# Toeplitz stage of an S5 layer: steps of four groups instead of two, state copies moved behind the low parts, and more column products behind the scan

## The chip, the cores and the metric

One NeuronCore of a Trainium2 chip runs the whole layer in one launch. The metric is the device time in microseconds (us) of an execution; the profile belongs to one such execution. PE is the matrix engine, DVE the vector engine, ACT the scalar engine, POOL the GpSimd engine and SP the engine that issues most DMAs.

## The reference

A bidirectional encoder layer over 2 sequences of 512 tokens, 1024 wide. A projection yields queries, keys, values, the state-space input u and two gates. The attention branch is windowed; the state-space branch (S5) runs a diagonal complex recurrence with 64 states for each of 64 groups of 16 channels, forwards and backwards, and applies GELU and a gated linear unit; then both are merged and a squared-ReLU MLP follows. The part that matters here:

```python
def one_direction(us, d, reverse):
    bu_re = jnp.einsum('lgc,gpc->lgp', us, bb_re[d])
    bu_im = jnp.einsum('lgc,gpc->lgp', us, bb_im[d])
    ...
    _, _, h_re, h_im = lax.associative_scan(_complex_combine, (ar, ai, bu_re, bu_im),
                                            reverse=reverse, axis=0)
    return (jnp.einsum('lgp,gcp->lgc', h_re, cr[d])
            - jnp.einsum('lgp,gcp->lgc', h_im, ci[d]))
...
y = one_direction(ug, 0, False) + one_direction(ug, 1, True)
y = jax.nn.gelu(y.reshape(seq_len, SSM_WIDTH) + dsk * uf)
```

## The kernel before

The recurrence is cut into chunks of 8 tokens. In a first stage (the tables) the kernel builds, for every group, a Toeplitz matrix that maps the 128 inputs of a chunk (16 channels x 8 tokens) to its outputs, and two tables of 128 columns (real and imaginary) that map the states at a chunk's edges to the outputs. Tables go to DRAM (`ct_scr`, L522, with 9 column blocks of 16, of which the Toeplitz stage uses 8; `lag_scr`, from which `toep_scr` is made). Then the scan walks over the 64 chunks on DVE (L602 to L605). Then comes the **Toeplitz stage**, with the loop that the change rewrites.

Before the change this loop has 32 turns `q`, each for two groups (`SH` = 2), which share one PSUM bank:

- PE: for each group one product of the Toeplitz matrix with the inputs (L642) and two of the tables with the states (L645). In the trace each of these f32 products is two records, so a turn has 12 of them.
- The states are copied out of the scan's array `h` into a tile `st`, in the order that the products read. `state_rows(q)` copies the partitions 64 to 127 on DVE (L613), and 0 to 63 on ACT for even q (L615) or on DVE for odd q (L617). There are three `st` buffers, and turn q makes the states of turn q + 2.
- ACT: GELU of the bank (L655), then the rounding to the matmul format, the high part (L621). DVE: the low part, the difference (L622). In the code the low part and the store of a turn stand one turn later, behind the state copies of that turn (`remainder`, `full`).
- ACT issues the stores of both parts to `y_scr` (L626) after every four groups (`SI` = 4). The part tiles have two buffers each, so a high part needs the store of two stores ago landed.
- POOL issues the loads: the state tables of four groups (L590, three buffers), and u and the Toeplitz matrices of eight groups (`SB` = 8; L582 and L584, two buffers).

On PE, ACT and DVE the code's order is the queue's order here (`manual_schedule`); POOL's and SP's order is chosen by a scheduler. Into PE's queue the kernel weaves **fillers**: products of the other projections, which are needed later. `pull(n)` takes n units of them. A product of a column block, L185, is worth two units, 24 make one result of 128 x 512; ACT copies that result out (L200), ACT rounds pieces of the next weights (L175, `c_hi`), and DVE forms their low parts (L176, `c_lo`). When the columns are done, the key products follow: L225, one unit each, 24 for one tile of 128 tokens. Such a tile is squared on ACT (L232), summed on DVE (L234), turned into a scale on POOL (L236, L237) and scaled on DVE (L238). A result is taken out of PSUM at the place in ACT's and DVE's order where its last product was pulled.

Each step of the scan pulls 15 units; behind the scan stands `pull(32)`; each turn of the Toeplitz loop pulls its share of what is left over 84 units; and after the loop comes the rest. After that the attention stage begins with products that need weights from SP (L980, L981, L813).

Of the kernel before, what the change touches and what calls it, by code (L numbers as in the profile page):

```python
# [12 lines left out]
F32 = mybir.dt.float32  # L13
F32R = mybir.dt.float32r
I32 = mybir.dt.int32
AF = mybir.ActivationFunctionType
# [3 lines left out]
P = 128  # L20
# [5 lines left out]
NSEQ = 2  # L26
# [12 lines left out]
GROUPS = 64  # L39
STATE = 64  # L40
CH = 16
T = 8
NCHUNK = SEQ // T
SB = 8
SI = 4
SG = 4
SH = 2
# [16 lines left out]
def hybrid_layer(ctx, tc, x, rel, onehot, w_qkv, w_ug, vectors, lam, coefs, w_glu, w_out, ln2,  # L64
                 w_up, w_down, out):
    nc = tc.nc
    V, S, PE, GP, SP = nc.vector, nc.scalar, nc.tensor, nc.gpsimd, nc.sync
# [4 lines left out]
    dram = ctx.enter_context(tc.tile_pool(name="dram", bufs=1, space=DRAM))  # L72
# [19 lines left out]
    ct_scr = dram.tile([P, GROUPS, 2, 9 * CH], F32, name="ct_scr")  # L92
# [58 lines left out]
    phase = {"next": 0, "raw": [], "units": 2 * 3 * KT * NSEQ * len(columns) + 3 * KT * NT, "gelu": False}  # L151
# [119 lines left out]
    with tc.tile_pool(name="xin", bufs=1, reuse_waits="tile") as xin, tc.tile_pool(name="ssmc", bufs=1) as sc:  # L271
# [148 lines left out]
        ps = ps_o.tile([P, 512], F32, tag="po", name="line")  # L420
# [21 lines left out]
    with tc.tile_pool(name="hst", bufs=1) as hp:  # L442
# [11 lines left out]
        with tc.tile_pool(name="ssmt", bufs=2) as sp:  # L454
# [9 lines left out]
            def tables(c):  # L464
# [22 lines left out]
                for q in range(SB // SG):  # L487
                    g0 = c * SB + q * SG
# [20 lines left out]
                    for ri, t in enumerate((bi_p, br_p)):  # L509
# [5 lines left out]
                    ctab = sp.tile([P, SG, 2, 9, CH], F32, tag="ctab", name="ctab")  # L515
# [3 lines left out]
                    V.tensor_sub(ctab[:, :, 0], tb, ctab[:, :, 0])  # L519
                    V.tensor_mul(ctab[:, :, 1], bc_pow(er, 9), bc_ch(cw[:, 1], 9))  # L520
                    V.tensor_sub(ctab[:, :, 1], ctab[:, :, 1], tb)
                    GP.dma_start(ct_scr[:, g0:g0 + SG].rearrange("p g r n -> p (g r n)"),  # L522
                                 ctab.rearrange("p g r n c -> p (g r n c)"))
# [54 lines left out]
        with tc.tile_pool(name="ssmo", bufs=2) as sp:  # L578
            def load_batch(g0):

                u_sb = sp.tile([P, SB, NSEQ * NCHUNK], F32, tag="u_sb", name="u_sb")
                GP.dma_start(u_sb, u_scr[g0:g0 + SB].rearrange("g c t k -> (c t) g k"))  # L582
                toep = sp.tile([P, SB, T, CH], F32, tag="toep", name="toep")
                GP.dma_start(toep.rearrange("p g t c -> p g (t c)"),  # L584
                             toep_scr[:, :, g0:g0 + SB].rearrange("c t g n -> (c t) g n"))
                return u_sb, toep

            def load_table(g0):
                ctab = sp.tile([P, SI, 2, 9 * CH], F32, tag="ctab", name="ctab_in", bufs=3)
                GP.dma_start(ctab.rearrange("p g r n -> p (g r n)"),  # L590
                             ct_scr[:, g0:g0 + SI].rearrange("p g r n -> p (g r n)"))
                return ctab

            ahead = [load_batch(0)]
            ahead_c = [load_table(0), load_table(SI), load_table(2 * SI)]
            ahead.append(load_batch(SB))
            GP.dma_start(line_scr, line_one[:, None, :].to_broadcast([N_HEADS, P, LINE]))
            order.close()
            order.enter_context(tc.manual_schedule(engines={mybir.EngineType.PE, mybir.EngineType.Activation, mybir.EngineType.DVE}))
            for i in range(1, NCHUNK - 1):  # L600
                t1, t2 = [sp.tile([P, 2, GROUPS, NSEQ], F32, tag="st", name=n, bufs=3) for n in ("t1", "t2")]
                V.tensor_mul(t1, h[:, i], a8r)  # L602
                V.tensor_mul(t2, h[:, i, ::-1], a8i)
                V.tensor_add(t1, t1, h[:, i + 1])
                V.tensor_add(h[:, i + 1], t1, t2)  # L605
                pull(15)
            phase["gelu"] = True
            pull(32)
            def state_rows(q):
                st = sp.tile([P, 2, SH, NSEQ, NCHUNK], F32, tag="st", name="st", bufs=3)  # L610
                hv = h[:, :, :, q * SH:(q + 1) * SH, :].rearrange("p k r g s -> p r (g s) k")
                sv = st.rearrange("p r g s k -> p r (g s) k")
                V.tensor_copy(sv[64:128], hv[64:128, :, :, ::-1])  # L613
                if q % 2 == 0:
                    S.copy(sv[0:64], hv[0:64])  # L615
                else:
                    V.tensor_copy(sv[0:64], hv[0:64])  # L617
                return st

            def rounded(y, parts, g):  # L620
                S.copy(parts[0][:, g:g + SH, :], y)  # L621
                return lambda: V.tensor_sub(parts[1][:, g:g + SH, :], y, parts[0][:, g:g + SH, :].bitcast(F32))  # L622
# [7 lines left out]
            remainder = full = None  # L630
            for q in range(GROUPS // SH):
                g0 = q * SH
                if g0 % SB == 0:
                    u_sb, toep = ahead.pop(0)
                if g0 % SI == 0:
                    ctab = ahead_c.pop(0)
                    ysp = [sp.tile([P, SI, NSEQ * NCHUNK], F32R, tag=f"y{n}", name=f"y{n}") for n in ("hi", "lo")]
                st = states.pop(0)
                ps = sps()
                for g in range(SH):  # L640
                    o = ps[:, g * P:(g + 1) * P]
                    PE.matmul(o, toep[:, g0 % SB + g].rearrange("p t c -> p (t c)"), u_sb[:, g0 % SB + g, :],  # L642
                              start=True, stop=False)
                    for ri in range(2):
                        PE.matmul(o, ctab[:, g0 % SI + g, ri, 0:T * CH],  # L645
                                  st[:, ri, g].rearrange("p s k -> p (s k)"), start=False, stop=ri == 1)
# [8 lines left out]
                S.activation(yg.rearrange("p g k -> p (g k)"), ps[:, 0:SH * P], AF.Gelu_apprx_tanh)  # L655
                remainder = rounded(yg, ysp, g0 % SI)
                if (g0 + SH) % SI == 0:
                    full = ysp, g0 + SH - SI

                pull(-(-(phase["units"] - 84) // (GROUPS // SH - q)))  # L660
                if (g0 + SH) % SI == 0 and g0 + SH + 2 * SI < GROUPS:
                    ahead_c.append(load_table(g0 + SH + 2 * SI))
                if (g0 + SH) % SB == 0 and g0 + SH + SB < GROUPS:
                    ahead.append(load_batch(g0 + SH + SB))
            remainder()
            store_y(*full)
            pull(phase["units"])
            order.close()

# [66 lines left out]
    with tc.tile_pool(name="att", bufs=2, reuse_waits="tile") as ap, tc.tile_pool(name="attc", bufs=1, reuse_waits="tile") as ac:  # L736
# [289 lines left out]
        with tc.manual_schedule(engines={ET.PE, ET.Activation, ET.DVE, ET.Pool}):  # L1026
            for i, (j, sq) in enumerate(steps):
# [152 lines left out]
    with tc.tile_pool(name="glu", bufs=1, reuse_waits="tile") as gpool, \  # L1180
# [10 lines left out]
        for u in range(2, 2 * KT):  # L1191
            m, s = divmod(u, 2)
# [206 lines left out]
    with tc.tile_pool(name="up", bufs=2, reuse_waits="tile") as fp:  # L1399
# [26 lines left out]
        for r in range(NPAIR):  # L1426
# [40 lines left out]
    with tc.tile_pool(name="downb", bufs=1, side="right", reuse_waits="tile") as db, \  # L1467
# [47 lines left out]
        ps = product_d(1)  # L1515
# [5 lines left out]
        ps = product_d(5)  # L1521
# [5 lines left out]
        ps = product_d(6)  # L1527
# [3 lines left out]
        ps = product_d(3)  # L1531
# [4 lines left out]
        ps = product_d(7)  # L1536
# [5 lines left out]
        ps = product_d(2)  # L1542
# [3 lines left out]
        ps = product_d(4)  # L1546
# [82 lines left out]
```

## Time and profile before

| What | us |
|---|---|
| median of 3 runs | 1474.6 |
| the runs | 1472.87 to 1474.95 |
| the profiled execution, its own time | 1474.1 |
| span of that execution in the trace | 1472.3 |
| scan (L602 to L605) in the trace | up to 323.3 |
| Toeplitz products (L642, L645) in the trace | 326.7 to 411.4 |
| last key product (L225) | about 422.4 |

A span begins with the first and ends with the last recorded instruction; the time holds what lies around it too. In lists of instructions the first number is the start in us from the span's start, the second the duration in us; "x4" counts records that were merged, and "[1.81 <-ACT st L615]" is idle time of the engine just before, with what ended it. In groups by line the columns are the line, engine and operation, output and inputs with shape and count, then busy us, mean ns, idle time in front and its causes. Matmuls are pipelined: the record of a matmul ends later than the start of the next.

### The profile page before, as it was taken

The page shows a single profiled execution, that of the slowest core. Times are in us where ns is not written, and L with a number is a line of the kernel's source. Part 1 is how long each engine was busy: PE and PEld are TensorE (multiplying, and loading weights), DVE is VectorE, ACT ScalarE, POOL GpSimd, SP SyncE. Part 2 cuts the span into 40 slices and gives each one's busy share as a digit, 9 for nine tenths or more (in the row PEclk, how much of TensorE's full clock was granted, in tenths as well). Part 3 has the DMA queues.
Part 4 walks back from the last instruction along what each step waited for, and adds up shares of the span by engine and source line. Part 5 has one row for each costly group of instructions (what it writes and reads, how often), then busy time and mean ns, then how long its engine had stood idle before and what let it go on. Part 6 is the DMA issues. An engine that isn't in the chain of part 4 may idle for free.

```text
span 1472.3 us, 22141 instructions
## 1 busy us (share of the span) xinstructions
PE 1442.3 (98%) x8074; PEld 1230.4 (84%) x8074; DVE 1101.7 (75%) x1989; ACT 760.0 (52%) x1362; POOL 210.4 (14%) x372
## 2 busy tenths in 40 slices
PE   6999999999999999999999999999999999999998
PEld 4788888879899999998888878888888888888787
DVE  7998859986645899997984588777776597475553
ACT  6677762225535888776343355544544444333332
POOL 3133351002322444222100000000000000000000
PEclk9999999999999999999999999999999999999999
DMA  4455459328940445367553244444443893454441
GB/s 177 142 172 172 165 167 362 116 100 299 346 163 16 144 151 158 107 234 232 191 193 114 86 157 175 148 153 145 146 150 115 326 338 108 158 184 146 127 129 58
DMA packets 102877, 249.16 MB, mean 169 GB/s; under 512 B 12234, under 2 KB 23754, under 8 KB 102768
## 3 DMA queue, kind: packets, MB, share of 16 engines
q1 hardware_dynamic: 60240, 139.55, 29.2%
q0 software_dynamic: 16896, 53.53, 10.5%
q10 hardware_dynamic: 25632, 54.67, 9.9%
q8 instruction: 64, 1.05, 0.3%
q14 instruction: 45, 0.37, 0.1%
HBM read 173.22 MB, written 90.21 MB: 179 GB/s over the span
## 4 chain that ended last, share of the span: by engine, by line
PE 82%; DVE 7%; ACT 4%; DMA 3%; issue 3%; POOL 1%; ACTq 0%; SPq 0%; DVEq 0%; POOLq 0%
PE acc L185 14%; PE bank L117 14%; PE bank L118 13%; PE bank L116 13%; PE acc L813 5%; PE acc L123 3%; PE acc L117 2%; PE acc L118 2%; PE acc L116 2%; PE po L896 2%; PE sps L864 2%; PE sps L547 2%; PE tps L880 2%; PE acc L835 1%; PE sps L645 1%
## 5 line engine op out<-in xcount | busy, mean ns | idle before, releaser
L185 PE MATMUL acc<-act,c_hi 128*128 128x512 f32 x768 | 250.5, 401 | 1.0 <-DVE act L304 0.9
L117 PE MATMUL bank<-b_lo,a_hi 128*128 128x512 f32 x448 | 174.6, 390 | 1.4 <-DVE b_lo L1498 1.4
L118 PE MATMUL bank<-b_hi,a_lo 128*128 128x512 f32 x448 | 174.3, 389 | 0.0
L116 PE MATMUL bank<-b_hi,a_hi 128*128 128x512 f32 x448 | 173.5, 389 | 0.0
L185 PEld LDWEIGHTS acc<-act,c_hi 128*128 128x128 f32 x768 | 142.6, 190 | 29.2 <-DVE act L304 2.4
L185 PE MATMUL acc<-act,c_lo 128*128 128x512 f32 x384 | 153.2, 399 | 0.0
L1497 ACT CAST a_hi<-d_a 128x1024 fp32r<-128x1024 f32 x56 | 59.0, 1054 | 179.3 <-PE bank L117 177.7
L116 PE MATMUL bank<-act,act 128*128 128x512 f32 x368 | 143.3, 389 | 0.5 <-ACT f_sum L1322 0.5
L117 PE MATMUL bank<-act,act 128*128 128x512 f32 x368 | 143.3, 389 | 0.2 <-DVE act L1281 0.2
L118 PE MATMUL bank<-act,act 128*128 128x512 f32 x368 | 143.2, 389 | 0.0
L1498 DVE TENSOR_TENSOR a_lo<-d_a,a_hi 128x1024 fp32r<-128x1024 f32 x56 | 68.5, 1224 | 99.7 <-ACT a_hi L1497 99.7
L813 PE MATMUL acc<-w_hi,act 128*128 128x256 f32 x512 | 114.2, 291 | 0.0
L117 PEld LDWEIGHTS bank<-b_lo,a_hi 128*128 128x128 f32 x448 | 84.1, 188 | 19.6 <-DVE b_lo L1498 2.4
L116 PEld LDWEIGHTS bank<-b_hi,a_hi 128*128 128x128 f32 x448 | 84.1, 188 | 17.6
L118 PEld LDWEIGHTS bank<-b_hi,a_lo 128*128 128x128 f32 x448 | 84.1, 188 | 17.4
L813 PEld LDWEIGHTS acc<-w_hi,act 128*128 128x128 f32 x512 | 87.1, 190 | 3.7
L185 PEld LDWEIGHTS acc<-act,c_lo 128*128 128x128 f32 x384 | 72.8, 190 | 14.0 <-DVE c_lo L176 0.5
L116 PEld LDWEIGHTS bank<-act,act 128*128 128x128 f32 x368 | 69.1, 188 | 15.3 <-ACT f_sum L1322 0.9
L117 PEld LDWEIGHTS bank<-act,act 128*128 128x128 f32 x368 | 69.1, 188 | 14.9 <-DVE act L1281 0.5
L874 ACT ACTIVATE p<-p,nmx 128x257 f32<-128x257 f32 (+1 forms) x128 | 72.1, 564 | 17.9 <-DVE nmx L868 16.7
L118 PEld LDWEIGHTS bank<-act,act 128*128 128x128 f32 x368 | 69.1, 188 | 14.2
L123 PE MATMUL acc<-act,gc_hi 128*128 128x512 f32 x256 | 80.8, 394 | 0.0
(332 smaller groups left out, 3422.1 us busy)
## 6 DMA issues: line engine op xcount, KB each, us to landing
d_a<-a_scr SPq DMA_DIRECT2D x56, 512.0 KB, 3.6
raws<-in_w_up_dram SPq DMA_DIRECT2D x32, 512.0 KB, 4.1
a_scr<-t ACTq DMA_DIRECT2D x64, 256.0 KB, 2.9
k<-in_w_down_dram SPq DMA_DIRECT2D x32, 512.0 KB, 6.1
c_raw<-in_w_ug_dram SPq DMA_DIRECT2D x48, 256.0 KB, 3.7
ct_scr<-ctab POOLq DMA_DIRECT2D x16, 576.0 KB, 3.7
ctab_in<-ct_scr POOLq DMA_DIRECT2D x16, 576.0 KB, 7.4
y_scr<-y_scr POOLq DMA_DIRECT2D x16, 512.0 KB, 5.5
```

Source lines behind the costliest of these rows:

```text
L116: PE.matmul(ps, a[0], b[0], start=first, stop=False)
L117: PE.matmul(ps, a[0], b[1], start=False, stop=False)
L118: PE.matmul(ps, a[1], b[0], start=False, stop=last)
L123: PE.matmul(ps, w[wi][:, k, :], rows[yi], start=k + p == 0, stop=k == KT - 1 and p == 2)
L185: PE.matmul(ps, w[wi][:, k, :], hT[s][hi][:, k, :], start=n == 0, stop=n == 3 * KT - 1)
L547: PE.matmul(ps[:, i * P:(i + 1) * P], bm[:, ri, g, :], u_sb[:, gp * SH + g, :], start=True, stop=True)
L813: PE.matmul(self.ps, hT[sq][act][:, k, col:col + P], w[:, k % 4, :], start=i == 0, stop=i == 3 * KT - 1)
L864: PE.matmul(ps[:, 0:self.nk], qs, kk[:, self.k0 * P:self.k1 * P], start=i == 0, stop=i == 1)
L874: S.activation(p, p, AF.Exp, bias=self.nmx[:, h:h + 1], scale=-1.0, accum_out=self.sums[:, h, self.qb:self.qb + 1])
L880: PE.transpose(pt[:, h * P:(h + 1) * P], self.p[:, h, 1 + i * P:1 + (i + 1) * P], ident)
L1497: S.copy(hi, src)
L1498: V.tensor_sub(lo, src, hi.bitcast(F32))
```

## The change

The table store keeps only the 8 blocks of columns that are used, and so the tables in DRAM and in SBUF shrink from 9 x 16 to 8 x 16 columns. u and the Toeplitz matrices are loaded for four groups at a time into four buffers instead of for eight into two. `st` has four buffers instead of three. Behind the scan 64 units are pulled instead of 32, and the two first states are copied behind these. The loop has 16 steps of four groups (two banks): first all Toeplitz products of the step, then half of its fillers, then GELU, high part and low part of both banks, then the copies of the next step's two states, then the stores, then the other half of the fillers, then the loads. What is kept back for after the loop rises from 84 to 108 units.

```diff
@@ tables @@
-                    GP.dma_start(ct_scr[:, g0:g0 + SG].rearrange("p g r n -> p (g r n)"),
-                                 ctab.rearrange("p g r n c -> p (g r n c)"))
+                    GP.dma_start(ct_scr[:, g0:g0 + SG].rearrange("p g r n -> p (g r) n"),
+                                 ctab[:, :, :, 0:T].rearrange("p g r n c -> p (g r) (n c)"))
@@ loads @@
-                u_sb = sp.tile([P, SB, NSEQ * NCHUNK], F32, tag="u_sb", name="u_sb")
-                GP.dma_start(u_sb, u_scr[g0:g0 + SB].rearrange("g c t k -> (c t) g k"))
-                toep = sp.tile([P, SB, T, CH], F32, tag="toep", name="toep")
+                toep = sp.tile([P, SI, T, CH], F32, tag="toep", name="toep", bufs=4)
...
+                u_sb = sp.tile([P, SI, NSEQ * NCHUNK], F32, tag="u_sb", name="u_sb", bufs=4)
+                GP.dma_start(u_sb, u_scr[g0:g0 + SI].rearrange("g c t k -> (c t) g k"))
...
-                ctab = sp.tile([P, SI, 2, 9 * CH], F32, tag="ctab", name="ctab_in", bufs=3)
+                ctab = sp.tile([P, SI, 2, T * CH], F32, tag="ctab", name="ctab_in", bufs=3)
...
-            pull(32)
+            pull(64)
...
-                st = sp.tile([P, 2, SH, NSEQ, NCHUNK], F32, tag="st", name="st", bufs=3)
+                st = sp.tile([P, 2, SH, NSEQ, NCHUNK], F32, tag="st", name="st", bufs=4)
@@ the loop @@
-            for q in range(GROUPS // SH):
...
-                if q + 2 < GROUPS // SH:
-                    states.append(state_rows(q + 2))
-                if remainder:
-                    remainder()
-                if full:
-                    store_y(*full)
-                    full = None
-                yg = sp.tile([P, SH, NSEQ * NCHUNK], F32, tag="yg", name="yg")
-                S.activation(yg.rearrange("p g k -> p (g k)"), ps[:, 0:SH * P], AF.Gelu_apprx_tanh)
-                remainder = rounded(yg, ysp, g0 % SI)
...
-                pull(-(-(phase["units"] - 84) // (GROUPS // SH - q)))
...
+            for b in range(GROUPS // SI):
...
+                for q in range(SI // SH):
+                    st = states.pop(0)
+                    ps = sps()
+                    banks.append(ps)
+                    for g in range(SH):
+                        o, k = ps[:, g * P:(g + 1) * P], q * SH + g
+                        PE.matmul(o, toep[:, k].rearrange("p t c -> p (t c)"), u_sb[:, k, :], start=True, stop=False)
+                        for ri in range(2):
+                            PE.matmul(o, ctab[:, k, ri, 0:T * CH],
+                                      st[:, ri, g].rearrange("p s k -> p (s k)"), start=False, stop=ri == 1)
+                pulled = -(-(phase["units"] - 108) // (GROUPS // SI - b))
+                pull(pulled // 2)
+                for q, ps in enumerate(banks):
+                    yg = sp.tile([P, SH, NSEQ * NCHUNK], F32, tag="yg", name="yg")
+                    S.activation(yg.rearrange("p g k -> p (g k)"), ps[:, 0:SH * P], AF.Gelu_apprx_tanh)
+                    rounded(yg, ysp, q * SH)()
+                if g0 + SI < GROUPS:
+                    states += [state_rows((g0 + SI) // SH + q) for q in range(SI // SH)]
+                store_y(ysp, g0)
+                pull(pulled - pulled // 2)
+                if g0 + 3 * SI < GROUPS:
+                    ahead_c.append(load_table(g0 + 3 * SI))
+                if g0 + 4 * SI < GROUPS:
+                    ahead.append(load_batch(g0 + 4 * SI))
```

The changed kernel is seven lines shorter from here on, so its line numbers differ: the table products are L644, the GELU is L650, the loads of toep and u_sb L582 and L585.

How the orders change shows on three engines. First DVE at the scan's end, with the last instruction of the scan (L605), the copies of states (L613, L617) and low parts (`c_lo` of weights, `ylo` of the stage's results). Before:

```order
L605 TENSOR_TENSOR h<-t_3537,t_3538 128x256
L613 COPY st<-h 64x512 x2
L617 COPY st<-h 64x512
L613 COPY st<-h 64x512
L176 TENSOR_TENSOR c_lo<-c_raw,c_hi 128x512
```

With the change:

```order
L605 TENSOR_TENSOR h<-t_3545,t_3546 128x256
L176 TENSOR_TENSOR c_lo<-c_raw,c_hi 128x512 x2
L613 COPY st<-h 64x512 x2
L617 COPY st<-h 64x512
L622 TENSOR_TENSOR ylo<-yg,yhi 128x256 x2
```

The first states' copies stand behind two low parts of weights, and the copies of the next states behind the low parts of the results.

Next DVE where the first key tile is taken out, late in the loop (L234 is the tile's sum, L238 its scaling). Before:

```order
L617 COPY st<-h 64x512
L622 TENSOR_TENSOR ylo<-yg,yhi 128x256
L234 TENSOR_REDUCE ms<-keys 128x4
L238 TENSOR_TENSOR keys<-acc,rk 128x256
L613 COPY st<-h 64x512
L622 TENSOR_TENSOR ylo<-yg,yhi 128x256
```

With the change:

```order
L613 COPY st<-h 64x512 x2
L617 COPY st<-h 64x512
L234 TENSOR_REDUCE ms<-keys 128x4
L238 TENSOR_TENSOR keys<-acc,rk 128x256
L622 TENSOR_TENSOR ylo<-yg,yhi 128x256 x2
L613 COPY st<-h 64x512 x2
L617 COPY st<-h 64x512
```

One state copy and one low part alternated; now both low parts of a step and then the three copies of the next step's states stand in a row, and a key tile's sum and scaling stand ahead of all five.

At the same place on ACT, L232 is the tile's square, L655 or L650 the GELU, L621 the high part, L626 the store. Before:

```order
L621 CAST yhi<-yg 128x256
L232 ACTIVATE keys<-acc 128x256
L615 COPY st<-h 64x512
L626 DMA y_scr<-yhi 128x512
L626 DMA y_scr<-ylo 128x512
L655 ACTIVATE yg<-sps 128x256
```

With the change:

```order
L615 COPY st<-h 64x512
L626 DMA y_scr<-yhi 128x512
L626 DMA y_scr<-ylo 128x512
L232 ACTIVATE keys<-acc 128x256
L650 ACTIVATE yg<-sps 128x256
L621 CAST yhi<-yg 128x256
```

The square stood behind the GELU and high part of its turn; now it stands ahead of the GELUs of the step in which the tile's last product lies. On POOL the load of u for the last step stands between L236 and L237 of this first key tile.

More of the change, by code (lines that the diff above doesn't have):

```diff
@@ L91, in hybrid_layer @@
     y2_scr = dram.tile([2, GROUPS, CH, T, NSEQ * NCHUNK], F32, name="y2_scr")
-    ct_scr = dram.tile([P, GROUPS, 2, 9 * CH], F32, name="ct_scr")
+    ct_scr = dram.tile([P, GROUPS, 2, T * CH], F32, name="ct_scr")
     toep_scr = dram.tile([CH, T, GROUPS, T * CH], F32, name="toep_scr")
@@ L579, in load_batch @@
             def load_batch(g0):
-                u_sb = sp.tile([P, SB, NSEQ * NCHUNK], F32, tag="u_sb", name="u_sb")
-                GP.dma_start(u_sb, u_scr[g0:g0 + SB].rearrange("g c t k -> (c t) g k"))
-                toep = sp.tile([P, SB, T, CH], F32, tag="toep", name="toep")
+                toep = sp.tile([P, SI, T, CH], F32, tag="toep", name="toep", bufs=4)
                 GP.dma_start(toep.rearrange("p g t c -> p g (t c)"),
-                             toep_scr[:, :, g0:g0 + SB].rearrange("c t g n -> (c t) g n"))
+                             toep_scr[:, :, g0:g0 + SI].rearrange("c t g n -> (c t) g n"))
+                u_sb = sp.tile([P, SI, NSEQ * NCHUNK], F32, tag="u_sb", name="u_sb", bufs=4)
+                GP.dma_start(u_sb, u_scr[g0:g0 + SI].rearrange("g c t k -> (c t) g k"))
                 return u_sb, toep
             def load_table(g0):
-                ctab = sp.tile([P, SI, 2, 9 * CH], F32, tag="ctab", name="ctab_in", bufs=3)
+                ctab = sp.tile([P, SI, 2, T * CH], F32, tag="ctab", name="ctab_in", bufs=3)
                 GP.dma_start(ctab.rearrange("p g r n -> p (g r n)"),
@@ L595, in hybrid_layer @@
             ahead_c = [load_table(0), load_table(SI), load_table(2 * SI)]
-            ahead.append(load_batch(SB))
+            ahead += [load_batch(i * SI) for i in range(1, 4)]
             GP.dma_start(line_scr, line_one[:, None, :].to_broadcast([N_HEADS, P, LINE]))
@@ L600, in hybrid_layer @@
             for i in range(1, NCHUNK - 1):
-                t1, t2 = [sp.tile([P, 2, GROUPS, NSEQ], F32, tag="st", name=n, bufs=3) for n in ("t1", "t2")]
+                t1, t2 = [sp.tile([P, 2, GROUPS, NSEQ], F32, tag="st", name=n, bufs=4) for n in ("t1", "t2")]
                 V.tensor_mul(t1, h[:, i], a8r)
@@ L629, in hybrid_layer @@
             states = [state_rows(0), state_rows(1)]
-            remainder = full = None
-            for q in range(GROUPS // SH):
[L632 to L646, printed above, removed]
-                if q + 2 < GROUPS // SH:
-                    states.append(state_rows(q + 2))
-                if remainder:
-                    remainder()
-                if full:
-                    store_y(*full)
-                    full = None
-                yg = sp.tile([P, SH, NSEQ * NCHUNK], F32, tag="yg", name="yg")
-                S.activation(yg.rearrange("p g k -> p (g k)"), ps[:, 0:SH * P], AF.Gelu_apprx_tanh)
-                remainder = rounded(yg, ysp, g0 % SI)
-                if (g0 + SH) % SI == 0:
-                    full = ysp, g0 + SH - SI
-                pull(-(-(phase["units"] - 84) // (GROUPS // SH - q)))
[L661 to L664, printed above, removed]
@@ L665, in hybrid_layer @@
-            remainder()
-            store_y(*full)
+            for b in range(GROUPS // SI):
+                g0 = b * SI
+                u_sb, toep = ahead.pop(0)
+                ctab = ahead_c.pop(0)
+                ysp = [sp.tile([P, SI, NSEQ * NCHUNK], F32R, tag=f"y{n}", name=f"y{n}") for n in ("hi", "lo")]
+                banks = []
+                for q in range(SI // SH):
[22 more added lines that the diff above has]
+                    ahead.append(load_batch(g0 + 4 * SI))
```

## The prediction

> **What bounds the kernel now.** I read the page first, for the engine that has no room.
>
> ```profile
> span 1472.3 us, 22141 instructions
> PE 1442.3 (98%) x8074; PEld 1230.4 (84%) x8074; DVE 1101.7 (75%) x1989; ACT 760.0 (52%) x1362; POOL 210.4 (14%) x372
> ```
>
> PE is busy for 98% of the span and the change leaves its matmuls as they are, so it can only win or lose time in which PE stands still or runs slowly. Next, a table by stretches from the scan's end to the last key product (columns: length, busy us and records of PE, PEld, DVE, ACT, POOL, then clock, DMA share, GB/s).
>
> ```profile
> 326.40:329.60 3.20, 1.39 (x11) 1.12 (x10) 0.02 (x1) 2.36 (x3) 0.00 (x0) 1.00 0.41 164
> 329.60:333.00 3.40, 3.40 (x14) 2.92 (x13) 0.46 (x1) 2.85 (x5) 0.00 (x0) 0.50 0.00 0
> 333.00:369.90 36.90, 36.90 (x254) 33.82 (x254) 25.39 (x41) 21.72 (x43) 9.90 (x14) 1.00 0.92 318
> 369.90:389.80 19.90, 19.55 (x156) 18.54 (x155) 13.36 (x23) 10.74 (x21) 6.34 (x11) 1.00 1.00 357
> 389.80:412.00 22.20, 19.36 (x162) 18.59 (x162) 13.29 (x24) 11.06 (x26) 5.34 (x10) 1.00 0.68 256
> ```
>
> PE is idle at the stage's start and its end, hardly between. The view of waits, for PE from 326 to 423 us (total, times, longest), names what ended it:
>
> ```profile
> PE sps L645 <- ACT st L615: 1.8, 1, 1.8
> PE sps L645 <- DVE st L617: 1.2, 1, 1.2
> PE sps L642 <- ACT yg L655: 1.0, 1, 1.0
> PE sps L642 <- ACT yhi L621: 0.6, 1, 0.6
> PE sps L642 <- DMA toep<-toep_scr: 0.4, 1, 0.4
> ```
>
> That is 5.0 us. A matmul record is 0.28 us long, but with nothing to wait for the next starts 0.11 us behind its start, so each wait costs about 0.16 us more: 5.8 us. The clock of 0.50 over 3.40 us behind the first wait costs another 1.7 us. **7.5 us is all that the stage can give back**, before the change adds anything.
>
> **What a step costs PE.** In the chain of work (start, us, what), one step of two groups with its fill:
>
> ```profile
> 335.55 0.22 PE sps L642 x2
> 335.77 0.45 PE sps L645 x4
> 336.22 0.22 PE sps L642 x2
> 336.44 0.45 PE sps L645 x4
> 336.89 1.15 PE acc L185 x5
> ```
>
> Two groups are 12 records and 1.34 us (0.112 each), an L185 product 0.23 us. A key product (L225) takes 0.12 us: 68 of them in 8.17 us.
>
> ```profile
> 411.40 8.17 PE acc L225 x68
> ```
>
> From the pull rule I count the fill of the changed kernel. At its first Toeplitz product 348 units are left (78 L185 at 2 units, 192 L225 at 1). With 108 kept back, steps 0 to 8 get 8 L185 each, step 9 six L185 and 3 L225, steps 10 to 12 14 L225, steps 13 to 15 13. So PE needs 2.68 + 8 x 0.23 = 4.52 us in a step of the first kind, 4.4 in step 9, 2.68 + 14 x 0.12 = 4.36 in the next three, 4.24 in the last.
>
> **The states' path, steps 0 to 14.** This decides the forecast. A state copy no longer depends only on a free buffer: on DVE the six instructions of a step stand as low part, low part, three copies, so the states of step b+1 wait for the GELU and the high part of step b. The durations, from the groups by line between 322 and 424 us (busy, mean ns):
>
> ```profile
> L655 ACT ACTIVATE yg<-sps 128x256 f32<-128x256 f32 x32 | 12.3, 384 | 33.2 <-PE sps L645 15.6 <-DVE ylo L622 12.1 <-PE acc L225 4.1
> L621 ACT CAST yhi<-yg 128x256 fp32r<-128x256 f32 x32 | 13.0, 407 | 2.0 <-DMA y_scr<-yhi 1.1
> L622 DVE TENSOR_TENSOR ylo<-yg,yhi 128x256 fp32r<-128x256 f32 x32 | 13.3, 418 | 4.0 <-DMA y_scr<-ylo 3.2
> L613 DVE COPY st<-h 64x512 f32<-64x512 f32 x32 | 24.6, 771 | 7.9 <-PE sps L645 7.2
> L617 DVE COPY st<-h 64x512 f32<-64x512 f32 x16 | 12.3, 766 | 0.2
> ```
>
> And what lies between PE and ACT, from the order of time on both engines:
>
> ```profile
> 338.76 0.61 PE L645 MATMUL sps<-st,ctab_in 128*128 128x128 f32 x4
> 339.13 0.48 PE L185 MATMUL acc<-act,c_lo 128*128 128x512 f32 x1
> 339.41 0.39 ACT L655 ACTIVATE yg<-sps 128x256 f32<-128x256 f32 x1 [0.43 <-PE sps L645]
> 339.83 0.41 ACT L621 CAST yhi<-yg 128x256 fp32r<-128x256 f32 x1
> ```
>
> GELU starts 0.28 us after PE has gone on to its next product, and the high part 0.42 after that. Let S be the moment at which PE leaves the Toeplitz products of step b. Then GELU of the second bank starts at S+0.28, its high part at 0.70 and ends at 1.11; the low part starts at 1.15 (0.04 from engine to engine), the first copy at 1.59, and three copies of 0.76 end at 3.87. At 3.91 the second bank of step b+1 can read its states; 10 of its 12 records are still to come, 1.12 us: PE leaves step b+1 at S+5.0. PE alone would have been done at S+4.52, so **each step with 8 L185 loses about 0.5 us**, nine of them 4.5; step 9 0.6, steps 10 and 12 0.65 each, step 14 0.75: 2.65. Together 7.1 us. Before, two states lay ready and this path was as long, but nobody stood behind it.
>
> **Two key tiles in the way, steps 11 and 13.** With these counts a key tile's last product is the 7th of step 11 and the 3rd of step 13, in the first half, so its square stands on ACT ahead of that step's GELUs and its reduction and scaling on DVE ahead of the low parts. What such a tile takes (start, us), in the kernel before:
>
> ```profile
> 414.02 0.39 ACT L232 ACTIVATE keys<-acc 128x256 f32<-128x256 f32 x1 [1.77 <-PE acc L225]
> 414.44 0.42 DVE L234 TENSOR_REDUCE ms<-keys 128x4 f32<-128x256 f32 x1 [0.84 <-ACT keys L232]
> 414.95 0.23 POOL L236 TENSOR_SCALAR ms<-ms 128x4 f32<-128x4 f32 x1 [2.48 <-DVE ms L234]
> 415.26 1.04 POOL L237 TENSOR_TENSOR rk<-ms,neg_half 128x4 f32<-128x4 f32 x1
> 416.34 0.42 DVE L238 TENSOR_TENSOR keys<-acc,rk 128x256 f32<-128x256 f32 x1 [1.47 <-POOL rk L237]
> ```
>
> 2.74 us from square to scaled keys, 1.5 of it with DVE waiting. In step 11 the 7th product ends at S+1.0, the keys are scaled at 3.75, two low parts later it is 4.63, three copies 6.9, and PE leaves the next step at 8.1 instead of 4.36: 3.7 us. In step 13 the tile ends at S+0.5: 7.6 against 4.24, 3.4 us. Together **7.1 us**. The third tile falls in step 15, which has no states behind it. In step 11 POOL's order puts a u_sb load between L236 and L237. These rows bound its issue, for eight groups and for a load in longer pieces:
>
> ```profile
> 389.05 0.97 POOL L582 DMA_DIRECT2D u_sb<-u_scr  x1 [1.27 <-PE sps L642]
> 390.60 0.65 POOL L584 DMA_DIRECT2D toep<-toep_scr  x1
> ```
>
> Four groups: between 0.5 and 1.0, and nothing if the reduction comes late; I take 0.5. The two c_lo ahead of step 10's low parts (0.69 each) cost 0 to 1.4, mostly while DVE waits: 0.4.
>
> **The clock.** Both long waits exceed the 1.97 us that brought half clock for 3.40 us, so a slow stretch is likely behind each: 0 to 1.7 us each, and as part of it falls into the step's own wait, 0.8 each, 1.6 in all. The Trainium skill, "TensorE: Matmul & The Clock Gate", section "HAM oscillation — how this bites in real kernels", puts the danger at idle gaps over about 3.4 us. This trace disagrees: 1.97 us was enough. By the page alone at most one of the two waits would be followed by a slow stretch, and the sum would be 0.8 us lower.
>
> **What is removed or hidden.** The start: 32 L185 (7.3 us) instead of 16 lie between scan and first product. On DVE two c_lo now stand before the copies, behind an ACT copy that ends at 327.07:
>
> ```profile
> 326.48 0.59 ACT L200 COPY sg<-acc 128x512 f32<-128x512 f32 x1 [4.84 <-PE acc L185]
> 327.10 0.33 ACTq L209 DMA_DIRECT2D gs_scr<-sg  x1
> 331.89 0.61 ACT L175 CAST c_hi<-c_raw 128x512 fp32r<-128x512 f32 x1
> ```
>
> Two c_hi end at 328.7 and ACT's state copy (1.09) at 329.8; two c_lo end at 329.4, DVE's first copy at 330.2. PE arrives at 330.1: the first wait and its slow clock go, 3.6 us of the 7.5; the second bank's copies end at 331.7 against 331.5. The toep wait goes with loads of half the size. The other waits are replaced by those worked out above, so I count all 7.5 as gone. Tables lose a ninth of their bytes, which only the DMA queues notice. The table store in 512-byte pieces may issue as slowly as that u_sb load, 16 x 0.4 = 6 us of POOL, which has time there:
>
> ```profile
> POOL ct_scr L522 <- DVE ctab L521: 54.8, 8, 10.9
> ```
>
> **Sum.** Paid: 7.1 + 7.1 + 0.5 + 0.4 + 1.6 = 16.7. Gone: 7.5. Net **+9.2 us**. The profiled execution took 1474.1 us (its span 1472.3 and 1.8 around it), half a microsecond below the median of the three: 1483.3.
>
> **Rivals.**
> - *The states still hide.* If the path after S were 0.5 us shorter, the steady loss would vanish. For it: the sum has margins of hundredths. Then 7.1 less is paid, and with the clock kept, 8.0 against 7.5: 1474.6, no change. 10%.
> - *Faster.* The same, and the key tiles' stalls hidden too: that needs the copies not to queue behind the scaling, against DVE's order. Paid nothing, 7.5 gained: 1466.6. It decides at a path of 3.4 us from S to the last copy, where I find 3.9. 8%.
> - *The stores come late.* A high part needs the store of two steps ago landed. The store leaves at about S+2.3, the buffer is wanted some 6.7 us later.
>
> ```profile
> y_scr<-yhi ACTq DMA_DIRECT2D x15, 256.0 KB, 6.3
> y_scr<-ylo ACTq DMA_DIRECT2D x15, 256.0 KB, 6.3
> ```
>
> The median just fits; landings of 8 us in half the steps would add 7 x 1.3 = 9 us: 1492. Against it: longer steps leave the queues more time. 8%.
> - *The longer cover does nothing*, if the extra c_lo wait: the start costs its 3.6 again, 1487. 6%.
>
> **How the numbers follow.** The forecast has 68%, from about 1476.5 (POOL, c_lo and clock at nothing, the steady loss at half) to 1488 (all at their upper ends). The range of 1474.5 to 1490 takes in half of the case of no change and leaves out the faster one and the late stores' upper part. A measurement tells 0.2%, 2.9 us: slower 82%, the same 10%, faster 8%.
>
> **What would show it.** On PE, 15 waits of 0.1 to 0.4 us on st by DVE, at both banks; two of over 3 us behind the key tiles of steps 11 and 13; no wait at 330 us, clock 1.00 there and 0.50 for 3.4 us behind the long ones; the last key product some 7 to 10 us later. It is wrong if PE's products follow each other every 4.5 us, or if the loss sits at a DMA.

## The result and the profile after

| | before | after |
|---|---|---|
| median, us | 1474.28 (1472.87 to 1474.95, 4 runs) | 1486.84 (1484.70 to 1487.64, 4 runs) |
| the profiled execution, us | 1474.11 | 1484.70 |
| end of the scan (last L605), us from the span's start | 323.3 | 322.0 |
| start of the first Toeplitz product | 326.7 | 329.1 |
| start of the last key product | 422.2 | 429.9 |

The ratio is 1.0088, 95% interval 1.0076 to 1.0100: the changed kernel is slower, by 12.6 us between the medians and by 10.6 us between the two profiled executions. The forecast was +9.2 us, and slower. Two executions in the experiments below ran at granted clocks of 0.705 and 0.743 and took 1919.61 and 1820.89 us; the medians and ratios there leave them out.

First the steady loss. The chain of waits of the kernel after, in the second of its steps (start us, us, what):

```profile
331.91 1.83 PE acc L185 x8
333.74 0.22 PE sps L642 x2
333.96 0.16 issue
334.12 0.68 PE sps L644 x4
...
336.87 1.84 PE acc L185 x8
```

From one L185 block to the next is 4.96 us, where PE's work alone is 4.51 (measured below, in a kernel without these waits). The hole stands behind the first Toeplitz product, which needs no state, and ahead of the first table product, which does. The view puts the cause at "issue"; in the view of the copies on ACT (L615) it is weight loads of L644 on PE that wait, 15 times. DVE's list of instructions at that place names what ended just then:

```profile
332.80 0.42 DVE L622 TENSOR_TENSOR ylo<-yg,yhi 128x256 fp32r<-128x256 f32 x1 [0.92 <-ACT yhi L621]
333.25 1.42 DVE L613 COPY st<-h 64x512 f32<-64x512 f32 x2
334.69 0.74 DVE L617 COPY st<-h 64x512 f32<-64x512 f32 x1
```

The list merges the two L613 copies; the first ends at 334.01, and PE's table product starts at 334.12; and L613 starts 0.03 us after the second low part is done. So low part, copy and table product form one chain through the step, as forecast. ACT's copy for the same product, behind the high part, ends only 0.22 us earlier, at 333.79, so a faster DVE alone would have ended only part of this wait. That the loss went unseen in the step times has a reason: the kernel before also took 4.97 us for four groups in most of the stage, but there ten L185 products stood in them and here eight: equal step times hid a different amount of work.

Then the key tile of step 11. DVE, POOL and PE of the kernel after:

```profile
387.83 0.42 DVE L234 TENSOR_REDUCE ms<-keys 128x4 f32<-128x256 f32 x1 [2.72 <-ACT keys L232]
390.55 0.42 DVE L238 TENSOR_TENSOR keys<-acc,rk 128x256 f32<-128x256 f32 x1 [2.30 <-POOL rk L237]
390.89 0.75 DVE L622 TENSOR_TENSOR ylo<-yg,yhi 128x256 fp32r<-128x256 f32 x2
391.67 1.38 DVE L613 COPY st<-h 64x512 f32<-64x512 f32 x2
```

```profile
388.34 0.23 POOL L236 TENSOR_SCALAR ms<-ms 128x4 f32<-128x4 f32 x1 [0.88 <-DVE ms L234]
388.64 0.79 POOL L585 DMA_DIRECT2D u_sb<-u_scr  x1
389.45 1.06 POOL L237 TENSOR_TENSOR rk<-ms,neg_half 128x4 f32<-128x4 f32 x1
```

```profile
388.12 0.49 PE L642 MATMUL sps<-u_sb,toep 128*128 128x128 f32 x2
392.50 0.99 PE L644 MATMUL sps<-st,ctab_in 128*128 128x128 f32 x4 [3.89 <-issue]
```

DVE stands still for 2.30 us on the scale, 0.79 of it for a load of u that POOL issues in between; then come two low parts and the copy, and PE has waited 4.06 us more than between such products elsewhere (start to start). Behind the tile of step 13 it is 3.07.

What the clock did, by windows (stretch, its length, PE busy, granted clock, DMA share, GB/s), at the start of the stage and behind each of the two long waits:

```profile
326.00:333.00 7.00, 7.00 (x45) 1.00 0.43 150
```

```profile
392.60:396.00 3.40, 3.40 (x17) 0.52 0.59 220
406.30:409.70 3.40, 3.24 (x15) 0.51 0.21 77
```

At the start no wait is left and the clock is full. Behind each long wait it is about half for 3.4 us. The Trainium skill, "TensorE: Matmul & The Clock Gate", section "HAM oscillation — how this bites in real kernels", speaks of gaps over about 3.4 us; by it the shorter wait, 2.91 us of idle time in the profile, would have been harmless. It was not.

### The profile page after: what moved, and what is told of

It is laid out like the page before. It is cut to its first block, busy times and chain, and to the rows that moved or that the text cites. A ratio compares the mean times of both kernels' runs of the same rounds, so it can differ in the third digit from the quotient of the medians.

```text
span 1482.9 us, 22173 instructions
## 1 busy us (share of the span) xinstructions
PE 1446.7 (98%) x8074; PEld 1233.5 (83%) x8074; DVE 1099.4 (74%) x1989; ACT 760.3 (51%) x1362; POOL 225.7 (15%) x388
## 3 DMA queue, kind: packets, MB, share of 16 engines
q0 software_dynamic: 17152, 51.43, 10.6%
## 4 chain that ended last, share of the span: by engine, by line
PE 86%; DVE 6%; ACT 3%; issue 2%; DMA 1%; POOL 0%; SPq 0%; ACTq 0%; DVEq 0%
PE acc L185 15%; PE bank L117 13%; PE bank L118 13%; PE bank L116 13%; PE acc L806 5%; PE acc L123 3%; PE acc L117 3%; PE acc L118 3%; PE acc L116 3%; PE sps L644 2%; PE po L889 2%; PE sps L857 2%; PE tps L873 2%; PE sps L547 2%; PE sps L642 1%
## 5 line engine op out<-in xcount | busy, mean ns | idle before, releaser
L185 PE MATMUL acc<-act,c_hi 128*128 128x512 f32 x768 | 248.4, 399 | 1.0 <-DVE act L304 1.0
L185 PEld LDWEIGHTS acc<-act,c_hi 128*128 128x128 f32 x768 | 142.2, 189 | 29.6 <-DVE act L304 2.4
L185 PE MATMUL acc<-act,c_lo 128*128 128x512 f32 x384 | 152.1, 396 | 0.0
L185 PEld LDWEIGHTS acc<-act,c_lo 128*128 128x128 f32 x384 | 72.4, 188 | 14.2 <-DVE c_lo L176 0.5
L867 ACT ACTIVATE p<-p,nmx 128x257 f32<-128x257 f32 (+1 forms) x128 | 72.1, 564 | 18.0 <-DVE nmx L861 16.7
```

What stands on the lines that cost most here:

```text
L185: PE.matmul(ps, w[wi][:, k, :], hT[s][hi][:, k, :], start=n == 0, stop=n == 3 * KT - 1)
L867: S.activation(p, p, AF.Exp, bias=self.nmx[:, h:h + 1], scale=-1.0, accum_out=self.sums[:, h, self.qb:self.qb + 1])
```

## The experiments

**The state copies moved.** If the copies' place behind the low parts causes the steady loss, taking them ahead must end it. In the first kernel they stand behind the first half of the fillers:

```diff
                 pull(pulled // 2)
+                if g0 + SI < GROUPS:
+                    states += [state_rows(...) ...]
                 for q, ps in enumerate(banks):
...
-                if g0 + SI < GROUPS:
-                    states += [state_rows(...) ...]
                 store_y(ysp, g0)
```

> The changed kernel with the copies of the next step's states ahead of the step's low parts, but still behind the first half of its fillers. Theory (the copies stand behind the low parts, so PE waits for them in every step): the 15 waits of 0.3 to 0.5 us on st go, 7.1 us; the key tiles' scaling still stands ahead of the copies in steps 11 and 13, two waits of 2 to 3 us stay; time about 1478 us, 9 below the changed kernel. Rival (the loss is the DMA's, late stores or loads): within 1 us of the changed kernel's 1487.

Measured: 1476.55 us, ratio 1.0024 (1.0014 to 1.0034). The profile is of another execution of the same kernel:

> The first experiment again, for a profile (states' copies ahead of the low parts but behind half of the fillers). Theory: no waits on st in the steps without a key tile; two waits of 2 to 3 us in steps 11 and 13, with or without half clock behind them.

That execution took 1477.89 us. Its first nine steps take 4.51 us each, from first Toeplitz product to first Toeplitz product: the steady loss is gone. Its view of waits on PE (326 to 440 us; engine, line, what it waited for, us, times, longest) shows what is left:

```profile
PE sps L644 <- DVE st L613: 3.6, 2, 2.2
PE sps L642 <- ACT yg L652: 1.4, 2, 0.9
```

Two waits on states, behind the two key tiles, whose sum and scaling still stand ahead of the copies on DVE. The two waits for a bank come just ahead of these: on ACT the step's GELUs stand behind the key tile's square and the state copy.

In the second kernel the same lines stand ahead of `pulled = ...`, so also ahead of the key tiles' instructions:

> The changed kernel with the copies of the next step's states ahead of the first half of its fillers too, so ahead of key tiles and low parts. Theory: both kinds of waits go, and the two stretches of half clock with them; what is left is the gain of 7.5 us that the stage could give back: about 1468 us, 6 below the kernel before. Rival (the steps of four groups themselves cost it, by PSUM banks or stores): PE still waits 0.3 us or more per step, time 1475 or more.

Measured: 1470.82 us, ratio 0.9983 (0.9973 to 0.9992). No wait on a state is left, and the chain holds work alone:

```profile
332.29 1.83 PE acc L185 x8
334.11 0.22 PE sps L642 x2
334.33 0.45 PE sps L644 x4
```

The repeat of the changed kernel (below) is 11.2 us above the kernel before that ran beside it, and this kernel is 2.7 us below its own: moving these two lines is worth 13.9 us. That is 2.7 us against the kernel before, not the 6 expected. What remains are waits for PSUM banks, 1.0 us at most (1.9 in three), because a GELU stands on ACT behind the store of a low part that comes late. The longest stands behind a key tile's scaling. In the other two, 0.58 and 0.34 us, no key tile is near: DVE held the low part back until an earlier store had landed. For the first of them, DVE and PE:

```profile
363.17 0.76 DVE L622 TENSOR_TENSOR ylo<-yg,yhi 128x256 fp32r<-128x256 f32 x2 [4.19 <-DMA y_scr<-ylo]
```

```profile
366.24 0.49 PE L642 MATMUL sps<-u_sb,toep 128*128 128x128 f32 x2 [0.58 <-ACT yg L652]
```

So late stores, a rival of the prediction, do cost something once the state copies are out of the way. Outside the stage this kernel loses another 2.1 us (see the last point on the prediction).

**All fillers behind the stores.** This moves the key tiles' instructions behind the copies and leaves the steady order as it is:

```diff
-                pull(pulled // 2)
                 for q, ps in enumerate(banks):
...
-                pull(pulled - pulled // 2)
+                pull(pulled)
```

> The changed kernel with all fillers of a step pulled behind the states' copies and stores instead of half of them ahead of the GELUs; PE's order is the same. Theory (key tiles ahead of low parts and copies cost two long waits): those two waits and both stretches of half clock go, 7 + 0.5 + 2 us; the steady waits of 0.3 to 0.5 us stay: about 1477 us. Rival (the key tiles' scaling costs the same wherever it stands): 1487.

Measured: 1479.29 us, ratio 1.0038 (1.0023 to 1.0053). The steps keep their 4.95 to 4.99 us, the two long waits are gone, and a new one has come where the key weights begin. PE, and the clock behind:

```profile
382.90 0.28 PE L225 MATMUL acc<-c_hi,act 128*128 128x256 f32 x1
385.40 0.38 PE L225 MATMUL acc<-c_hi,act 128*128 128x256 f32 x1 [2.22 <-ACT c_hi L175]
```

```profile
384.00:388.00 4.00, 2.26 (x10) 0.72 0.94 320
```

A high part of the key weights now stands on ACT behind the state copy, the stores and a store of gates, and comes 2.22 us late; that wait, too, brings about half clock (0.55 over the 3.4 us from 385.4).

**The key tiles' places moved by a number.** With 116 units kept back in place of 108, their last products fall into other halves:

```diff
-                pulled = -(-(phase["units"] - 108) // (GROUPS // SI - b))
+                pulled = -(-(phase["units"] - 116) // (GROUPS // SI - b))
```

> The changed kernel with 116 units kept back for after the loop instead of 108: by the pull rule the key tiles then end in the second halves of steps 11, 13 and 15. Nothing else changes. Theory (a tile costs its wait where it ends ahead of a step's GELUs): the two long waits and both stretches of half clock go, 9 us; the steady waits stay and grow by 0.1 to 0.2 us in some steps: about 1478 us. Rival (a key tile costs the same anywhere in the loop): 1487.

Measured: 1476.08 us, ratio 1.0014 (1.0005 to 1.0024). Waits on PE, and the stretch with the key products:

```profile
PE sps L644 <- ACT st L615: 3.0, 6, 0.8
PE acc L117 <- DVE w_lo L974: 1.3, 1, 1.3
```

```profile
378.00:410.00 32.00, 28.90 (x235) 1.00 0.79 288
```

The steady steps stay at 4.96 to 4.99 us; no wait on a state exceeds 0.99 us start to start, and the clock stays full. A change of one number in the count of fillers is worth 9.0 us against the repeat of the changed kernel below. What it moved is where two reductions fall in the order of DVE and ACT.

**64 units behind the scan, in the kernel before.**

```diff
-            pull(32)
+            pull(64)
```

> The kernel before with 64 units behind the scan instead of 32, nothing else. Theory: the first wait of 1.97 us and the half clock behind it go, 3.6 us: about 1470.7 us. Rival (two low parts of weights now stand ahead of the first copies, and the wait only moves): 1474, a wait of over 1 us at the first Toeplitz product.

Measured: 1475.92 us, ratio 1.0013 (1.0003 to 1.0023), not the gain expected. The start's wait goes, but PE reaches the loads earlier. PE's waits on these loads, and the place of one of the two:

```profile
PE sps L642 <- DMA toep<-toep_scr: 4.8, 2, 2.5
```

```profile
359.40 0.39 PE L185 MATMUL acc<-act,c_hi 128*128 128x512 f32 x1
362.30 0.46 PE L642 MATMUL sps<-u_sb,toep 128*128 128x128 f32 x2 [2.51 <-DMA toep<-toep_scr]
```

Loads of eight groups in two buffers land too late for a stage that starts without its pause, and the granted clock behind this wait was 0.61 over 3 us. So the gain seems to have been turned into a new wait. To test that, the same with the change's loads of four groups in four buffers:

```diff
-                toep = sp.tile([P, SB, T, CH], F32, tag="toep", name="toep")
+                toep = sp.tile([P, SI, T, CH], F32, tag="toep", name="toep", bufs=4)
...
-            pull(32)
+            pull(64)
```

> The kernel before with 64 units behind the scan and with u and the Toeplitz matrices loaded for four groups into four buffers, as the change does; loop, order and table as before. In the run with 64 units alone PE waited 4.8 us for two toep loads of eight groups. Theory (the shorter turns need the loads earlier, and the small loads come earlier): these waits go, 1470 to 1471 us. Rival (the DMA queues are full, so the size doesn't matter): 1475 to 1476.

Measured: 1473.34 us, ratio 0.9995 (0.9986 to 1.0004). No wait on toep is left, and counted from the scan's end the last key product comes 2.03 us earlier than before (96.87 us against 98.90). The time falls short of the 1470 to 1471 us expected, and a difference from the kernel before is not shown; what was won shows partly as other waits:

```profile
PE sps L641 <- ACT yg L654: 2.4, 2, 1.4
PE acc L225 <- DVE c_lo L176: 1.5, 1, 1.5
```

**The changed kernel once more**, in one series with the runs of 116 units, of the small loads and of the parts put together:

> The changed kernel once more, for a second profile. Theory: 15 waits of 0.3 to 0.6 us and two of 3 to 4 us on st come back at the same places to a tenth of a microsecond, since they follow from the order and the durations; time about 1487 us. Where this execution is slower than the first profiled one (1484.7), the difference lies outside the Toeplitz stage. Rival (chance meetings of DMAs make the waits): places and lengths differ.

Measured: 1485.12 us (1484.07 to 1485.71), ratio 1.0076 (1.0061 to 1.0091). The waits come at the same places with the same lengths: nine of 0.29 to 0.32 us, then 0.40, 0.46, 4.05, 0.47, 3.07 and 0.57.

**Parts put together.** Early copies, 116 units kept, three buffers for the results' parts and three in place of four for the loads:

```diff
-                ysp = [sp.tile(..., name=f"y{n}") for n in ("hi", "lo")]
+                ysp = [sp.tile(..., name=f"y{n}", bufs=3) for n in ("hi", "lo")]
```

> The changed kernel with the next states' copies ahead of all fillers of a step, 116 units kept back, and three buffers instead of two for the high and low parts (room for it from three instead of four buffers of u and the Toeplitz matrices). In the run with the copies ahead of the fillers alone, PE still waited 1.9 us for GELUs, behind low parts that waited for stores to land. Theory: these go too, about 1468 us, 2.5 below that run. Rival (loads with three buffers come late): waits on toep or u_sb by DMA, 1471 or more.

Measured: 1471.44 us, ratio 0.9988 (0.9978 to 0.9997). That is not shown to differ from early copies alone (0.9973 to 0.9992), and it is the rival's time, not the 1468 us of the theory. The waits for banks are gone, but a load of u came late. POOL issued it here, and it took 10.0 us to land; PE waited for it:

```profile
377.67 0.75 POOL L585 DMA_DIRECT2D u_sb<-u_scr  x1
```

```profile
387.80 0.46 PE L642 MATMUL sps<-u_sb,toep 128*128 128x128 f32 x2 [1.02 <-DMA u_sb<-u_scr]
```

With three buffers POOL can issue a load only a step later than with four; in the changed kernel, with four, PE never waited for one. PE then waits 0.64 us on a state, and here the parts work against each other: with 116 units kept back the key tile ends in the second half of a step, so its scaling stands just ahead of the next step's early copies. DVE:

```profile
387.68 0.42 DVE L238 TENSOR_TENSOR keys<-acc,rk 128x256 f32<-128x256 f32 x1 [3.48 <-POOL rk L237]
388.12 1.38 DVE L613 COPY st<-h 64x512 f32<-64x512 f32 x2
```

**The table's size in DRAM.** The changed kernel loses more time behind the stage than in the forecast, partly in waits on loads of the last stage. As the smaller table shifts the DRAM tensors behind it by 1 MB, two kernels keep the old size, the changed one and the one with early copies:

```diff
-    ct_scr = dram.tile([P, GROUPS, 2, T * CH], F32, name="ct_scr")
+    ct_scr = dram.tile([9, P * GROUPS * 2 * CH], F32, name="ct_scr")[0:T]...
```

> The changed kernel with the table in DRAM allocated at its old size and the first eight ninths of it used, so that all later DRAM tensors lie at the addresses of the kernel before; the loads and stores have the same sizes as in the changed kernel. All profiles with the smaller table show a wait of 1.2 to 1.8 us for a w_down load in the last stage (0.4 or none in those with the old size). Theory (the shift of addresses makes that load late): the wait falls to 0.4 or less and the time by 1 to 1.5 us, to about 1484.5. Rival (it is the moment at which the stage runs, or chance): the wait stays over 1.2 us.

> The run with the states' copies ahead of the fillers, with the table's old size in DRAM. If the addresses cost 1 to 1.5 us: about 1469.5, 4.5 below the kernel before. If not: 1471, as without.

Measured: 1485.66 us, ratio 1.0078 (1.0063 to 1.0094), for the changed kernel, and 1468.05 us (1467.38 to 1470.98), ratio 0.9966 (0.9954 to 0.9979), for early copies. The latter is faster than both kernels. PE's waits from 1150 to 1270 us, in the last stage, for the kernels before, after, and with early copies and the old size:

```profile
PE bank L117 <- DVE b_lo L1498: 0.2, 1, 0.2
```

```profile
PE bank L117 <- DVE b_lo L1491: 1.6, 1, 1.6
```

```profile
PE bank L118 <- DVE b_lo L1492: 1.4, 2, 1.2
```

The profile of the changed kernel with the old size has no such wait, but its time is no shorter (1485.66 us against 1485.12), and the profile of early copies with the old size has the wait. So the addresses alone do not decide it, as far as one profile each can tell; the latter is of the slowest of five executions. The interval of early copies with the old size (0.9954 to 0.9979) overlaps that with the small table (0.9973 to 0.9992), so that the old size is faster is not shown either.

The changed kernel with the old size had one wait more in the stage, in step 7, 1.1 us longer than its like. DVE there:

```profile
365.19 0.76 DVE L623 TENSOR_TENSOR ylo<-yg,yhi 128x256 fp32r<-128x256 f32 x2 [3.14 <-DMA y_scr<-ylo]
```

This is the rival of the late stores. In the three profiles of this loop DVE waits over 1 us for a store twice each, but this is the only time that PE waits longer for it.

## Why the prediction was right

Its terms can be read from the times between the steps' first Toeplitz products, against the kernel with early copies and the old size, which does the same products in the same steps (its own two waits, 0.44 and 1.13 us, taken off; for steps 1 to 8 its undisturbed 4.51 us is used):

| interval ended or held up by | forecast, us | measured, us |
|---|---|---|
| steps 1 to 9, copies behind low parts | 4.5 | 8 x 0.46 + 0.47 = 4.15 |
| steps 10, 11, 13 and 15, the same | 0.6 + 0.65 + 0.65 + 0.75 = 2.65 | 0.56 + 0.49 + 0.50 + 0.60 = 2.15 |
| step 12, behind the first key tile | 3.7 + 0.5 + 0.8 = 5.0 | 10.22 - 4.46 = 5.76 |
| step 14, behind the second | 3.4 + 0.8 = 4.2 | 8.97 - 4.30 = 4.67 |
| c_lo ahead of step 10's low parts | 0.4 | not seen apart |
| sum | 16.75 | 16.7 |

- **The steady loss** stood where it was forecast, and ended when the copies were moved. Its size was 0.46 us a step, not 0.5. Of this PE waits 0.31 ahead of the first bank's table products; two short delays follow, 0.07 within the first bank and 0.06 at the second, whose copies the prediction took to decide.
- **The key tiles.** The waits alone were 4.06 and 3.07 us against 4.2 (with POOL's load) and 3.4: right in place, a little high in size. POOL's load took 0.79 us, not 0.5. Moving their place by a number left no such wait over 1 us, as the theory asks.
- **The clock** was mis-sized: 0.8 us was counted behind each wait, because part of the slow stretch was thought to fall into the step's own wait. The two intervals hold 1.7 and 1.6 us more than wait and work, nearly all of the 1.7 that half clock over 3.4 us costs. This error of +1.7 us in all cancels the terms that were too high: 0.35 and 0.5 in the steady steps, 0.14 and 0.33 in the long waits, 0.4 for c_lo. The causes and their places were right; that the two sums agree to a tenth of a microsecond is luck.
- **The gone 7.5 us.** From the scan's end to the last key product the changed kernel takes 9.07 us more (429.91 - 321.95 against 422.15 - 323.25), so 16.7 - 9.07 = 7.6 went. This is what is left over, not a measurement of its own; that the start's wait and its slow clock are gone is seen in the trace. There the prediction read PE's arrival 0.3 us too early: its own rows give 326.7 + 16 x 0.23 = 330.4, not 330.1, so the copies had more room than it counted with. The step on toep was right, and it mattered more than the prediction said: without the smaller loads, the longer cover alone gave nothing.
- **The tables' store** issues in 0.91 us in place of 0.57, 16 times. It is hidden: POOL waits for the tables on both sides, as forecast. Kernel before, then after (duration in ns, least, median, most):

```profile
L522 POOL DMA_DIRECT2D ct_scr<-ctab x16: 538/566/602, 60.4 to 197.5; - x16
```

```profile
L522 POOL DMA_DIRECT2D ct_scr<-ctab x16: 890/906/987, 59.2 to 196.3; - x16
```

- **Outside the stage** the prediction counted nothing, and this is where the sum fell short: it put the rest of the kernel at nothing without a reason. From the last key product to the last product of all the changed kernel loses another 2.8 us in its profile and 2.7 in the repeat: 0.65 at the attention's first weights, some 0.6 spread over the next stages, and 1.4 to 1.6 in the last stage. Between profiled executions, +9.07 + 2.8 - 1.3 (the scan ended earlier in this one) is the 10.6 measured. The two kernels that keep the old loop lose 0 and 0.35 us there, and those with the new loop between 0.4 and 2.8. What in the new loop passes this on to later stages stays open; that it is the size of the table in DRAM is not borne out. The medians differ by 2 us more than the profiles, since the profiled execution of the changed kernel was the fastest of its four.
- **The range.** By the terms and bounds that the prediction names, the ends of its 68% come out at about 1477.3 and 1486.6 us, not at 1476.5 and 1488; the measured median lies just above the upper one, by what was lost outside the stage.

The rivals: states that still hide, the faster case and the longer cover without effect are refuted by the nine steady waits and the full clock at the start; late stores cost the changed kernel nothing that its two profiles show, and 1.1 us once in the one with the old table size.

## What to carry to other kernels

Where the code's order is an engine's order, as on PE, ACT and DVE here, ask of each moved instruction what it now stands behind: here a copy that the next step needs stood behind work that only a store needs, and moving it ahead again was worth some 14 us. A gain at the start of a stage has to be followed to the next thing that can be late, here a load of twice the size. And a reduction that crosses three engines belongs behind whatever the next step waits for, and a single count of fillers can decide where it falls.

## What the runs showed of the hardware

The lengths of single waits do not tell in every case whether half clock follows. One idle stretch of 1.47 us on PE (64 units with small loads, at 378.5 us) left the granted clock at 1.00, one of 2.22 us (late weights) did not. But in the kernel of the parts put together, stretches of 1.02 and 0.64 us close behind each other sufficed, and in the one with the copies ahead of the low parts 0.55 and 1.37 us (clock 0.60 over the 3.4 us from 400.4). The windows of the former (columns as above):

```profile
387.00:389.00 2.00, 0.56 (x3) 1.00 1.05 419
389.00:393.00 4.00, 4.00 (x22) 0.57 1.03 399
```

PE was idle for 1.44 of 2 us, and then ran at little more than half clock. This fits idle time that is summed over a stretch of time, not the longest gap, but no run was made to tell where its bound lies, or whether the moment of the idle time counts too. The two waits of about 3 and 4 us in the changed kernel cost nearly the same on top, 1.6 to 1.7 us each, in both of its profiles. That is no fixed price: in the changed kernel with the old table size the clock behind the first, equally long wait was 0.50 over the 4.6 us from 395.4, and the wait cost 2.7 us on top.
